# A dense SwiGLU trunk on one core: the down projection's first loads ahead of three products, their casts spread, and a bank order swapped

## The chip, the cores and the metric

The kernel runs on one core of one Trainium2 chip. The metric is the device time of one execution in microseconds, lower is better. TensorE (PE) multiplies, VectorE (DVE) and ScalarE (ACT) do elementwise work, GpSimd (POOL) does more of it from SBUF alone, and SyncE (SP) issues most of the transfers. TensorE writes into banks of PSUM, from which VectorE and ScalarE read.

## The reference

Two layers over a sequence of 1024 tokens of width 1024. Each layer has an attention part and a dense part. The change lies in the dense part:

```python
h = rmsnorm(x, norm_ffn[i])
gu = h @ w_gate_up[i]                                   # 1024 -> 2 * 2816
x = x + (silu(gu[..., :D_FF]) * gu[..., D_FF:]) @ w_down[i]   # 2816 -> 1024
```

All data are float32. The kernel keeps float32 accuracy by splitting every operand into a high part (a cast, on ScalarE, line L106) and a low part (operand minus high part, usually on VectorE, line L109), and runs three matmuls per product: high by high, high by low, low by high.

## The kernel before

**Gate and up.** The 22 column blocks of 128 are walked in pairs. `Pair(j)` is one block with its gate and up weights, and its share of the product is formed by a Strassen-like scheme of seven products, numbered 0 to 6, each of 12 matmuls of 128x512 (line L885). Results gather in two PSUM banks, X (products 0, 2, 4, 6) and Y (1, 3, 5). From block 4 on the seventh product of two neighbouring blocks is replaced by an object `Fourth`, which does it with a second Strassen step in quarters, split into three steps: "A", "B" and "C". Each step has six 128x256 matmuls per part (line L967), and gathers in two further banks, again named X and Y. So a pair (a, b) runs as a0 to a5, b0 to b3, A, b4, B, b5, C: the list `order`. After each product comes `read(n)`: for A and B two subtractions on VectorE (line L995), for C several more and the multiplication with the gate. A bank is written again only after its reading: A's banks by B, B's banks by C. `prepare` makes the weights of the product four steps ahead. After C, `hand_over` forms seven right-hand sides for the down projection and stores them in DRAM, `b_d` (line L1124).

**Down projection.** It, too, runs as seven products, numbered i, over the 11 pairs of rows, in six groups g of two rows (the last of one). For each (i, g):

- `keep_rows(g)` loads rows of the down weights (`wd_kept`, line L1178) once; they are kept for later products. Their tiles have tag "t8", six buffers, shared with operands of gate and up (the right sides of products 2, 3, and the one of A, B and C).
- `left_side(i, g)` casts these rows into high and low part (`wd`). These tiles share three buffers with the weights of gate and up.
- `right_side(i, g)` loads a piece of `b_d` into `b_raw` (line L1232) and casts its two halves into high and low part (`hB`). Both kinds of tile have tag "h", sixteen buffers, which the right sides of products 0, 1, 4 and 5 hold up to the last pair.

The matmuls of the down projection are line L1300.

**The order of the work.** `gate_up()` yields after each product with the number of products still to go, negative: -9 stands behind b0 of the last pair, -8 behind b1, -7 behind b2, -6 behind b3, -5 behind A, -4 behind b4, -3 behind B, -2 behind b5 and -1 behind C. At these places the loop below it starts the first groups of the down projection. The framework that builds the program puts each engine's instructions into one queue, in an order that it plans, and adds the semaphores; a tile gets its buffer in the order in which tiles of its tag are asked for.

Of the kernel before, what the change touches and what calls it, by code (L numbers as in the profile page):

```python
# [9 lines left out]
F32 = mybir.dt.float32  # L10
F32R = mybir.dt.float32r
AF = mybir.ActivationFunctionType
ALU = mybir.AluOpType
# [4 lines left out]
P = 128  # L18
# [3 lines left out]
HS = 512  # L22
# [19 lines left out]
def trunk_kernel(ctx: ExitStack, tc: tile.TileContext, a: dict, out: bass.AP):  # L42
# [21 lines left out]
    hp = pool("hp", bufs=16)  # L64
# [36 lines left out]
    def raw_tile(name):  # L101

        return phase[0].tile([P, D], F32, tag="raw", name=name, bufs=phase[2])

    def hi(dst, src):
        nc.scalar.copy(dst, src)  # L106
# [42 lines left out]
    def run_some(g, n):  # L149
        for _ in range(n):  # L150
            next(g, None)
# [119 lines left out]
    with tc.tile_pool(name="mp", bufs=1, reuse_waits="tile") as mp:  # L271
# [19 lines left out]
        for k in range(NK):  # L291
            t, g = mhl[:, k], gains[:, 4, k : k + 1]
# [24 lines left out]
        for i in range(8):  # L317
            l, u = divmod(i, 4)
# [47 lines left out]
    for layer in range(2):  # L366
        is_a = layer == 0
        with tc.tile_pool(name=f"ap{layer}", bufs=1, reuse_waits="tile") as ap:
# [385 lines left out]
            groups = 13  # L754
            for i in range(len(halves)):
# [12 lines left out]
                ahead = halves[min(i + 3, len(halves) - 1)].h  # L768
# [25 lines left out]
        with (  # L794
# [129 lines left out]
            h2 = HS // 2  # L924

            class Fourth:
# [45 lines left out]
                def product(self, n):  # L972
                    a11, a12, a22, s1, s2, s3, s4 = self.w
                    block = lambda k0, c: [
                        [B[6][k0 + k][:, i, c : c + h2] for i in range(2)] for k in range(2)
                    ]
                    b11, t1, b21, b22 = block(0, 0), block(0, h2), block(2, 0), block(2, h2)
                    t2, t3, t4 = ([[z[:, k] for z in t] for k in range(2)] for t in fourth)
                    if n == "A":
                        self.X = ps_t.tile([P, HS], F32, tag="T", name="X4")  # L980
                        self.Y = ps_o.tile([P, HS], F32, tag="O", name="Y4")
                        self.part(self.X, 0, a11, b11, start=True)
                        self.part(self.Y, 0, a12, b21, start=True)
                    elif n == "B":
                        self.part(self.X, 0, s2, t2)
                        self.part(self.Y, h2, s1, t1)
                    else:
                        self.part(self.X, 0, s3, t3)
                        self.part(self.Y, h2, s4, b22, stop=True)
                        self.part(self.X, h2, a22, t4, stop=True)  # L990

                def read(self, n):
                    (a, b), X, Y = self.units, self.X, self.Y
                    low, high = slice(0, h2), slice(h2, HS)
                    sub = lambda c, ps, op=ALU.subtract: nc.vector.tensor_tensor(c, c, ps, op=op)  # L995
                    if n == "A":
                        sub(a.c1[:, low], X[:, low])
                        sub(a.c1[:, low], Y[:, low])
                    elif n == "B":
                        sub(a.c1[:, high], X[:, low])  # L1000
                        sub(b.c1[:, high], Y[:, high])
                    else:
                        sub(
                            b.c1.rearrange("p (n c) -> p n c", n=2),
                            X[:, low].unsqueeze(1).to_broadcast([P, 2, h2]),
                        )
                        sub(a.c1[:, high], Y[:, high])
                        sub(b.c1[:, low], X[:, high], ALU.add)
                        for u in self.units:
                            sub(u.c1, u.g1, ALU.mult)  # L1010

            us = [Pair(j) for j in range(NF)]
            first = 4
# [14 lines left out]
            def load_gu():  # L1028
                u, i = next(loads, (None, 0))
                if u is not None:  # L1030
                    u.raw[i] = raw_tile("wgu_raw")
                    nc.sync.dma_start(u.raw[i], a["w_gu"][layer, 2 * u.j + i])
# [3 lines left out]
            for f in range(2):  # L1036
                for m in range(NK):
                    n = f * NK + m + 3
# [111 lines left out]
            def gate_up():  # L1150
                run_some(rest, 1)
                load_gu()
                for i, (u, n) in enumerate(order):
                    if i + lead < len(order):
                        v, n_ = order[i + lead]
                        v.prepare(n_)
                    u.product(n)
                    u.read(n)
                    run_some(rest, 1 if i < 2 * first else 2)
                    if i >= 7 * first - 1:  # L1160
                        run_some(more, 1)
                    if n == "C":
                        hand_over(u.units[0].j // 2, *u.units)
                    elif n == 6 and u.j % 2:
                        hand_over(u.j // 2, us[u.j - 1], u)
                    yield i - len(order)
# [3 lines left out]
            groups = [(p, min(2, HF - p)) for p in range(0, HF, 2)]  # L1170
# [5 lines left out]
            def rows(dst, g, i, cs):  # L1176
                p, n = groups[g]
                nc.sync.dma_start(dst, wd[p : p + n, i].rearrange("n r c -> r n c")[:, :, cs])  # L1178

            def keep_rows(g):  # L1180
                if g not in kept:
                    p, n = groups[g]
                    kept[g] = fp.tile([P, 2, 2, HS], F32, tag="t8", name="wd_kept", bufs=6)[:, :n]
                    rows(kept[g][:, :, 0], g, 0, slice(0, HS))

            def left_side(i, g):

                p, n = groups[g]
                first_cols, second_cols = slice(0, HS), slice(HS, D)

                def raw():
                    return raw_tile("wd_raw").rearrange("p (n c) -> p n c", c=HS)[:, :n]

                if i == 0:
                    keep_rows(g)
                a, b = kept[g][:, :, 0], kept[g][:, :, 1]
                if i == 0:
                    src = a
                elif i == 1:
                    src = raw()  # L1200
                    rows(src, g, 1, first_cols)
                elif i == 2:
                    nc.vector.tensor_tensor(a, b, a, op=ALU.subtract)
                    src = a
                elif i == 3:
                    r, o = raw(), raw()
                    rows(r, g, 0, second_cols)
                    rows(o, g, 1, second_cols)
                    nc.vector.tensor_tensor(b, r, o, op=ALU.add)
                    src = b  # L1210
                elif i == 4:
                    src, o = raw(), raw()
                    rows(src, g, 0, first_cols)
                    rows(o, g, 0, second_cols)
                    nc.vector.tensor_tensor(src, src, o, op=ALU.subtract)
                elif i == 5:
                    src = raw()
                    rows(src, g, 1, first_cols)
                    nc.vector.tensor_tensor(src, src, a, op=ALU.subtract)
                else:  # L1220
                    src = raw()
                    rows(src, g, 1, second_cols)
                w = wp.tile([P, 2, D], F32R, tag="whl", name="wd", bufs=3)
                hi(two(w[:, 0], n), src)
                lo(two(w[:, 1], n), src, two(w[:, 0], n))
                for q in range(n):
                    left[i, p + q] = w[:, :, q * HS : (q + 1) * HS]

            def right_side(i, g):
                p, n = groups[g]  # L1230
                raw = hp.tile([P, 2, HS], F32R, tag="h", name="b_raw").bitcast(F32)
                nc.sync.dma_start(  # L1232
                    raw[:, :n], b_d[layer][i][:, p * HS : (p + n) * HS].rearrange("r (n c) -> r n c", c=HS)
                )
                for q in range(n):
                    t = hp.tile([P, 2, HS], F32R, tag="h", name="hB")
                    hi(t[:, 0], raw[:, q])
                    lo(t[:, 1], raw[:, q], t[:, 0])
                    right[i, p + q] = t
# [65 lines left out]
            def finish(norm, at):  # L1305
# [23 lines left out]
                if last:  # L1329
                    nc.scalar.dma_start(out[:2].rearrange("k p t -> p k t")[:, :, at:], first)  # L1330

            for to_go in gate_up():
                if -7 <= to_go <= -5:
                    keep_rows(to_go + 7)
                    if to_go > -7:
                        left_side(0, to_go + 6)
                if -6 <= to_go <= -4:
                    right_side(0, to_go + 6)
            norms = [Norm(), Norm() if is_a else Norm(HS, 7)]
            dorder = [(i, g) for i in (0, 1, 3, 2, 4, 5, 6) for g in range(len(groups))]  # L1340
            parts = iter(())
# [1 line left out]
            for at_, (i, g) in enumerate(dorder):  # L1343
# [4 lines left out]
                p, n = groups[g]  # L1348
                if g == 0:
                    if i in (0, 6):  # L1350
                        X = banks(i)
# [114 lines left out]
```

## Time and profile before

| | us |
|---|---|
| median of 3 runs | 2156.2 |
| lowest, highest | 2154.42, 2159.33 |
| profiled execution, its own time | 2163.15 |
| span of the profiled execution | 2161.3 |

| engine | busy us | share of the span |
|---|---|---|
| PE | 2114.2 | 98% |
| PEld (weight loads, beside PE) | 1758.0 | 81% |
| DVE | 1514.0 | 70% |
| ACT | 1060.8 | 49% |
| POOL | 578.5 | 27% |

A row of the timeline has the start in us, the time, the engine, the line, the operation, the tiles written and read, the shapes and the count; a bracket has the engine's idle time before it and what ended that. Tiles are shown by name without number, so X, Y, `hB` and `wgu` stand for several tiles each; the line tells the products apart. The granted clock of TensorE is given as a share of full speed; its mean over the execution is 0.988.

### The profile page before, as it was taken

Reading aid. Unit: us, or ns where it says so; the run is one execution under the profiler, and the core shown is the slowest. Engines: PE = TensorE matmul, PEld = TensorE weight load, DVE = VectorE, ACT = ScalarE, POOL = GpSimd, SP = SyncE. Lnnn points to the kernel's source line nnn. Section 1 sums busy time; section 2 is a strip of 40 time slices with the busy share of each in tenths; the row PEclk is TensorE's granted clock in tenths of the full one; section 3 lists DMA queues with packets and bytes.
Section 4 is the critical chain, followed back from the end, with each engine's and each line's share of the span. In section 5 each row is a group of like instructions: output and inputs, shape, how many; then the busy total and the mean of one; then the engine's idle time right before and its main releaser. Section 6 shows DMA issues by size and latency. Waiting matters only on the chain. (4 is left out here: it accounts for less than half of the span.)

```text
span 2161.3 us, 28955 instructions
## 1 busy us (share of the span) xinstructions
PE 2114.2 (98%) x10270; PEld 1758.0 (81%) x10270; DVE 1514.0 (70%) x2466; ACT 1060.8 (49%) x2034; POOL 578.5 (27%) x617
## 2 busy tenths in 40 slices
PE   7999999999999999999999999999999999999997
PEld 6788888788888888888778888887888888878886
DVE  7677787788666666866766666677886666667675
ACT  6577785444433434334466566653543434344442
POOL 0344330334443430000233223203243444400000
PEclk9999999999999999999999999999999999999998
DMA  6321118323222336865232222274232333267662
GB/s 247 100 93 45 35 59 293 116 83 126 103 89 103 108 112 239 288 220 204 96 98 65 71 66 81 71 261 148 74 108 103 108 113 107 88 239 254 203 209 92
DMA packets 120081, 287.27 MB, mean 133 GB/s; under 512 B 12289, under 2 KB 18689, under 8 KB 119937
## 3 DMA queue, kind: packets, MB, share of 16 engines
q1 hardware_dynamic: 112896, 272.57, 37.4%
q10 hardware_dynamic: 7040, 12.85, 1.6%
q8 instruction: 81, 1.33, 0.3%
q14 instruction: 64, 0.52, 0.1%
HBM read 210.40 MB, written 68.94 MB: 129 GB/s over the span
## 5 line engine op out<-in xcount | busy, mean ns | idle before, releaser
L885 PE MATMUL Y<-hB,wgu 128*128 128x512 f32 x1056 | 261.6, 398 | 0.8 <-ACT c L905 0.8
L885 PE MATMUL X<-hB,wgu 128*128 128x512 f32 x1056 | 254.6, 390 | 0.0
L109 DVE TENSOR_TENSOR wgu<-wS,wgu 128x1024 fp32r<-128x1024 f32 (+1 forms) x124 | 153.4, 1237 | 130.5 <-ACT wgu L106 130.4
L1300 PE MATMUL X<-hB,wd 128*128 128x512 f32 x1056 | 242.3, 390 | 1.1 <-DVE x L1268 1.1
L885 PEld LDWEIGHTS Y<-hB,wgu 128*128 128x128 f32 x1056 | 200.4, 192 | 45.3 <-issue 1.9
L1300 PEld LDWEIGHTS X<-hB,wd 128*128 128x128 f32 x1056 | 197.9, 188 | 43.1 <-issue 2.4
L885 PEld LDWEIGHTS X<-hB,wgu 128*128 128x128 f32 x1056 | 196.1, 188 | 40.0
L587 POOL TENSOR_SCALAR p<-p,stat 128x384 f32<-128x384 f32 (+1 forms) x256 | 141.6, 573 | 313.1 <-DVE stat L584 203.7
L139 PE MATMUL mm<-hT,wqk 128*128 128x512 f32 x672 | 200.0, 405 | 0.1
L106 ACT CAST wgu<-wS 128x1024 fp32r<-128x1024 f32 (+1 forms) x124 | 114.3, 923 | 148.0 <-POOL wS L842 124.6
L139 PE MATMUL po<-yT,wo 128*128 128x512 f32 x768 | 184.6, 394 | 0.0
L1300 PE MATMUL Y<-hB,wd 128*128 128x512 f32 x792 | 180.4, 389 | 0.0
L233 POOL TENSOR_TENSOR nr<-nv,neg_half 128x4 f32<-128x4 f32 (+1 forms) x11 | 11.7, 1065 | 606.6 <-DVE nv L232 606.5
L1300 PEld LDWEIGHTS Y<-hB,wd 128*128 128x128 f32 x792 | 148.6, 188 | 31.1 <-DVE x L1268 0.3
L139 PEld LDWEIGHTS po<-yT,wo 128*128 128x128 f32 x768 | 142.4, 188 | 29.5 <-issue 1.0
L885 PE MATMUL X<-hT,wgu 128*128 128x512 f32 x624 | 150.2, 391 | 0.0
L842 POOL TENSOR_TENSOR wS<-wgu_raw 128x512 f32<-128x512 f32 x44 | 61.0, 1387 | 299.6 <-DVE wgu L109 299.6
L106 ACT CAST hB<-b_raw 128x512 fp32r<-128x512 f32 x154 | 88.9, 618 | 104.6 <-DMA b_raw<-b_d 87.4
L885 PEld LDWEIGHTS X<-hT,wgu 128*128 128x128 f32 x624 | 116.8, 188 | 26.3
L574 ACT ACTIVATE p<-p,stat 128x256 f32<-128x256 f32 (+1 forms) x192 | 112.4, 586 | 51.6 <-DVE stat L570 49.0
L109 DVE TENSOR_TENSOR pl<-pT,ph 128x384 fp32r<-128x384 f32 (+1 forms) x256 | 118.8, 494 | 21.3 <-ACT ph L106 18.4
L109 DVE TENSOR_TENSOR hB<-b_raw,hB 128x512 fp32r<-128x512 f32 x154 | 99.7, 687 | 46.9 <-ACT hB L106 46.9
(179 smaller groups left out, 4243.0 us busy)
## 6 DMA issues: line engine op xcount, KB each, us to landing
wgu_raw<-in_w_gu SPq DMA_DIRECT2D x92, 512.0 KB
wd_raw<-in_w_dn SPq DMA_DIRECT2D x70, 512.0 KB
b_raw<-b_d SPq DMA_DIRECT2D x70, 512.0 KB
b_d<-c SPq DMA_DIRECT2D x88, 256.0 KB
b_d<-t SPq DMA_DIRECT2D x66, 256.0 KB
wo_raw<-in_w_out SPq DMA_DIRECT2D x32, 512.0 KB
x<-in_x SPq DMA_DIRECT2D x32, 256.0 KB
xr_d<-x ACTq DMA_DIRECT2D x32, 256.0 KB
```

Of the source, the lines that this page charges most:

```text
L106: nc.scalar.copy(dst, src)
L109: (eng or nc.vector).tensor_tensor(dst, src, h.bitcast(F32), op=ALU.subtract)
L139: nc.tensor.matmul(ps[:, :n], l, r, start=start and i == 0 and j == 0, stop=stop and i == len(order) - 1 and j == 2,)
L233: nc.gpsimd.tensor_tensor(r[:, :nb], v[:, :nb], neg_half[:, :nb], op=ALU.pow)
L574: nc.scalar.activation(p[:, :n], p[:, :n], AF.Exp, bias=m1, scale=-1.0, accum_out=s1)
L587: nc.gpsimd.tensor_scalar(p[:, :n], p[:, :n], ri[:, i : i + 1], 1.0, op0=ALU.mult, op1=ALU.mult)
L842: sub = lambda o, p_, q_: nc.gpsimd.tensor_tensor(o, p_, q_, op=ALU.subtract)
L885: nc.tensor.matmul(ps, l, r, start=n in (0, 1, 3, 6) and k == 0 and i == 0, stop=k == 3 and i == 2, skip_group_check=True,)
L1300: nc.tensor.matmul(bank, l, r, start=i in (0, 1, 3, 6) and p == 0 and n == 0, stop=p == HF - 1 and n == 2, skip_group_check=True,)
```

## The change

Three edits.

1. In step C of `Fourth` the two parts that go to bank X run one after the other, and the part for bank Y comes last. `read("C")` follows: the two subtractions from X and the multiplication for block b first, then the subtraction from Y and the multiplication for block a.
2. `right_side` is split: `load_rows(i, g)` asks for the `b_raw` tile and starts its load; `right_side` does so only where it has not been done.
3. The start of the down projection within the last pair goes by a table. Before and after, by place:

| behind | before | after |
|---|---|---|
| b0 (-9) | | b_raw loads of groups 0 and 1 |
| b1 (-8) | | b_raw load of group 2 |
| b2 (-7) | kept rows 0 | kept rows 0, kept rows 1, casts of right side 0 |
| b3 (-6) | kept rows 1, left side 0, right side 0 | kept rows 2 |
| A (-5) | kept rows 2, left side 1, right side 1 | left side 0 |
| b4 (-4) | right side 2 | casts of right side 1 |
| B (-3) | | left side 1 |
| b5 (-2) | | casts of right side 2 |

```diff
                     else:
                         self.part(self.X, 0, s3, t3)
+                        self.part(self.X, h2, a22, t4, stop=True)
                         self.part(self.Y, h2, s4, b22, stop=True)
-                        self.part(self.X, h2, a22, t4, stop=True)
...
+                        sub(b.c1[:, low], X[:, high], ALU.add)
+                        sub(b.c1, b.g1, ALU.mult)
                         sub(a.c1[:, high], Y[:, high])
-                        sub(b.c1[:, low], X[:, high], ALU.add)
-                        for u in self.units:
-                            sub(u.c1, u.g1, ALU.mult)
+                        sub(a.c1, a.g1, ALU.mult)
...
-            def right_side(i, g):
+            raws = {}
+
+            def load_rows(i, g):
                 p, n = groups[g]
-                raw = hp.tile([P, 2, HS], F32R, tag="h", name="b_raw").bitcast(F32)
+                raws[i, g] = raw = hp.tile([P, 2, HS], F32R, tag="h", name="b_raw").bitcast(F32)
                 nc.sync.dma_start(
                     raw[:, :n], b_d[layer][i][:, p * HS : (p + n) * HS].rearrange("r (n c) -> r n c", c=HS)
                 )
+
+            def right_side(i, g):
+                p, n = groups[g]
+                if (i, g) not in raws:
+                    load_rows(i, g)
+                raw = raws.pop((i, g))
...
+            ahead = {
+                -9: [(load_rows, 0), (load_rows, 1)],
+                -8: [(load_rows, 2)],
+                -7: [(keep_rows, 0), (keep_rows, 1), (right_side, 0)],
+                -6: [(keep_rows, 2)],
+                -5: [(left_side, 0)],
+                -4: [(right_side, 1)],
+                -3: [(left_side, 1)],
+                -2: [(right_side, 2)],
+            }
             for to_go in gate_up():
-                if -7 <= to_go <= -5:
-                    keep_rows(to_go + 7)
-                    if to_go > -7:
-                        left_side(0, to_go + 6)
-                if -6 <= to_go <= -4:
-                    right_side(0, to_go + 6)
+                for what, g in ahead.get(to_go, ()):
+                    what(g) if what is keep_rows else what(0, g)
```

## The prediction

> **What bounds the kernel.** I read the page's busy shares first, then the timeline of TensorE where a pair of gate and up ends, then VectorE, ScalarE and SyncE there, and last the stretches with the granted clock.
>
> ```profile
> span 2161.3 us, 28955 instructions
> PE 2114.2 (98%) x10270; PEld 1758.0 (81%) x10270; DVE 1514.0 (70%) x2466; ACT 1060.8 (49%) x2034; POOL 578.5 (27%) x617
> ```
>
> TensorE bounds it; only time in which TensorE waits or runs slowly can be won. The next rows are TensorE at the last pair of layer 1: products A, b4 (L885, X), B (X, then Y), b5, C, and the first product of the down projection. Brackets are idle time and its releaser.
>
> ```profile
> 1915.00 0.88 PE L967 MATMUL X<-hT,wgu 128*128 128x256 f32 x6
> ...
> 1920.87 0.98 PE L967 MATMUL X<-q4h,wgu 128*128 128x256 f32 x6 [1.53 <-DVE c L995]
> 1923.89 1.65 PE L967 MATMUL Y<-hT,wgu 128*128 128x256 f32 x6 [2.05 <-DVE c L995]
> 1925.34 4.88 PE L885 MATMUL Y<-hB,wgu 128*128 128x512 f32 x12
> 1930.05 0.88 PE L967 MATMUL X<-q4h,wgu 128*128 128x256 f32 x6
> ...
> 1932.20 1.09 PE L1300 MATMUL X<-hB,wd 128*128 128x512 f32 x4
> ```
>
> From the start of A to the down projection: 1932.20 - 1915.00 = 17.20 us. The pair before it is the yardstick:
>
> ```profile
> 1876.88 0.88 PE L967 MATMUL X<-hT,wgu 128*128 128x256 f32 x6
> ...
> 1885.25 0.88 PE L967 MATMUL X<-q4h,wgu 128*128 128x256 f32 x6
> 1886.21 0.98 PE L967 MATMUL Y<-hT,wgu 128*128 128x256 f32 x6
> ...
> 1887.75 0.63 PE L885 MATMUL X<-hB,wgu 128*128 128x512 f32 x2
> ```
>
> A to C takes 1885.25 - 1876.88 = 8.37 us, and a C that waits for nothing 1932.20 - 1930.05 = 2.15. So 10.52 us would do, and the last pair of layer 1 loses 6.68. Layer 0 has the same place:
>
> ```profile
> 826.40 0.88 PE L967 MATMUL X<-hT,wgu 128*128 128x256 f32 x6
> ...
> 831.72 0.98 PE L967 MATMUL X<-q4h,wgu 128*128 128x256 f32 x6 [0.98 <-DVE c L995]
> 833.19 1.10 PE L967 MATMUL Y<-hT,wgu 128*128 128x256 f32 x6 [0.49 <-DVE c L995]
> ...
> 840.49 0.85 PE L1300 MATMUL X<-hB,wd 128*128 128x512 f32 x3
> ```
>
> 840.49 - 826.40 = 14.09: 3.57 lost. Why VectorE is late (layer 1; brackets name what ScalarE and VectorE waited for):
>
> ```profile
> 1914.06 0.57 ACT L902 COPY g<-X 128x512 f32<-128x512 f32 x1
> 1916.76 1.15 ACT L106 CAST hB<-b_raw 128x512 fp32r<-128x512 f32 x2 [2.14 <-DMA b_raw<-b_d]
> 1918.17 1.05 ACT L106 CAST wd<-wd_kept 128x1024 fp32r<-128x1024 f32 x1 [0.27 <-DMA wd_kept<-in_w_dn]
> 1919.13 0.58 ACT L905 COPY c<-Y 128x512 f32<-128x512 f32 x1
> 1919.26 1.23 DVE L109 TENSOR_TENSOR wd<-wd_kept,wd 128x1024 fp32r<-128x1024 f32 x1 [0.55 <-ACT wd L106]
> 1920.40 0.41 DVE L995 TENSOR_TENSOR c<-c,X 128x256 f32<-128x256 f32 x1
> 1921.20 1.05 ACT L106 CAST wd<-wd_kept 128x1024 fp32r<-128x1024 f32 x1 [1.50 <-DMA wd_kept<-in_w_dn]
> 1922.28 1.23 DVE L109 TENSOR_TENSOR wd<-wd_kept,wd 128x1024 fp32r<-128x1024 f32 x1 [1.47 <-ACT wd L106]
> 1923.42 0.41 DVE L995 TENSOR_TENSOR c<-c,Y 128x256 f32<-128x256 f32 x1
> 1923.75 0.69 DVE L893 TENSOR_TENSOR c<-c,c 128x512 f32<-128x512 f32 x1
> ```
>
> The subtractions that free A's two banks (L995) stand in VectorE's queue behind the low parts of group 0 and group 1 of the down projection's left side, which wait for ScalarE's casts, which wait for transfers. B may not overwrite the banks until then. The queues do not follow the program text: the copy L905 belongs to a product ahead of A, yet two casts written behind it run first. What counts is the built order, which I infer but cannot see: an operation seems to stand where its data were expected, and the data come later. SyncE's issues:
>
> ```profile
> 1904.76 0.93 SPq L1178 DMA_DIRECT2D wd_raw<-in_w_dn  x2
> 1905.79 0.42 SPq L1232 DMA_DIRECT2D b_raw<-b_d  x1
> 1909.25 0.34 SPq L1124 DMA_DIRECT2D b_d<-c  x1
> 1909.68 0.39 SPq L1249 DMA_DIRECT2D xr<-xr_d  x1
> 1910.15 0.42 SPq L1232 DMA_DIRECT2D b_raw<-b_d  x1
> 1911.11 3.09 SPq L1178 DMA_DIRECT2D wd_kept<-in_w_dn  x3
> 1914.25 0.46 SPq L1232 DMA_DIRECT2D b_raw<-b_d  x1
> ```
>
> The second b_raw was issued 4.4 us after the first, behind a store that waits for VectorE and a residual load. Last, the clock, and the transfers:
>
> ```profile
> 414.05:417.46 3.41, 2.51 (x16) 1.92 (x15) 2.12 (x3) 0.59 (x1) 3.04 (x2) 1.00 0.50 192
> 417.46:420.87 3.41, 3.41 (x9) 2.01 (x7) 0.69 (x1) 0.00 (x0) 1.02 (x1) 0.50 0.00 0
> 960.20:963.60 3.40, 2.35 (x11) 1.71 (x10) 3.40 (x6) 2.09 (x3) 0.00 (x0) 1.00 0.54 161
> 963.60:967.00 3.40, 3.40 (x17) 2.82 (x16) 3.19 (x5) 0.00 (x0) 0.00 (x0) 1.00 0.91 313
> 833.88:837.30 3.42, 3.42 (x11) 2.74 (x10) 1.72 (x4) 0.22 (x1) 0.00 (x0) 0.50 0.96 331
> 1919.00:1924.00 5.00, 1.42 (x9) 0.89 (x7) 3.28 (x5) 2.62 (x5) 0.00 (x0) 0.87 1.04 401
> ```
>
> Columns: stretch, us, busy PE, PEld, DVE, ACT, POOL, clock, DMA share, GB/s. Behind layer 0's stall TensorE runs at half clock for 3.42 us, which costs 1.7. A stretch with 3.41 - 2.51 = 0.90 us of idling (414.05) was followed by half clock, one with 3.40 - 2.35 = 1.05 (960.20) was not. The transfers are full at 401 GB/s: one of 0.52 MB takes 1.31 us.
>
> **C takes its second bank last.** In the yardstick C takes 1887.75 - 1885.25 = 2.50 us instead of 2.15: its Y part starts at 1886.21, 0.96 after the X part instead of 0.72. This grouped row (weight loads in layer 0's gate and up; layer 1's is the same) counts it:
>
> ```profile
> PEld Y L967 <- DVE c L995: 2.3, 8, 0.3
> ```
>
> 16 times 0.35 = 5.6 us. With both X parts first, Y starts at 1885.25 + 1.44 = 1886.69, 0.48 after the bank was free. Nothing else changes on TensorE. On VectorE the same five operations run in another order, b's bank first; who waits for them is hand_over and its stores to b_d, and in all pairs but the last those are read tens of us later, in the down projection. I take 5.6; bounds 0 (the late producer slips on with it) and 5.6.
>
> **The loads.** All three b_raw loads are written ahead of the pair's other transfers: two after b0, one after b1. Their slots come from operand tiles that b0 and b1 free one by one. Before, the second load's slot stood in line behind the first group's two cast tiles; now the three are next to each other. So on SyncE they should go out together near 1906, 0.42 us each in a queue idle until 1909.25, ahead of the store, the residual and the kept rows. The kept rows themselves wait for tiles that b2 and b3 free, so their issue at 1911.11 stays, whatever the text says. Bytes are the same. The three issues, 1.3 us together, are hidden in that idle stretch; if an operand tile came free late, SyncE would hold the store and the residual behind the waiting load, and neither is read before the down projection. The store's reader is group 5, the last. The change touches no queue of POOL.
>
> **The casts.** Right side 0 comes one product sooner, left side 0 behind A's read, the others later. ScalarE casts the three b_raw groups (3 * 1.15 us) in its idle time up to 1916, where today it stands 2.14 us waiting for the second; each low part follows on VectorE, which no one waits for there. Then I expect A's subtractions ahead of left side 0 on VectorE, so B starts when b4 ends. Gain up to 3.57 + 6.68 = 10.25 us. Late next: left side 1. Its kept rows landed at 1921.20 in layer 1; cast 1.05, low part 1.23, the addition that follows b4 (L893) 0.69 and B's subtraction 0.41 make 1924.6, while C would start at 1915.00 + 8.37 = 1923.37: 1.2 us of stall, and perhaps a half clock, 1.7. Layer 0 loses 3.1 us less today at the same queue order, so its transfers must come that much sooner, and I put its rest at none. Bounds of this rest: 0 to 2.9; I take 1.5, since 1.2 lies just above where the clock did and did not drop.
>
> In the Trainium skill ("TensorE: Matmul & The Clock Gate", Part 1: The HAM clock gate) the clock drops after an idle window of about 3.4 us. The trace disagrees: half clock followed 0.98 + 0.49 us of idling. By that rule the rest would be 1.2 and the sum 0.3 us larger.
>
> The skill's "DMA: Bandwidth & Descriptors" (Queues, rings and completion order) says that each engine consumes descriptors in ring order. That speaks against the change: the third b_raw, now ahead of the kept rows, would push them back by 1.31 us, and the sum would be that much smaller. In the trace the first kept rows landed only 1.4 us behind the second b_raw (1918.17 against 1916.76), which agrees; that they lose what the b_raw loads win is not shown.
>
> **Sum.** 5.6 + 10.25 - 1.5 = 14.35 us. The profiled execution took 2163.15 (span 2161.3), the median run 2156.2, so 6.95 less; where, no row tells. If a usual run loses in layer 1 what layer 0 loses, the gain is 5.6 + 2 * 3.57 = 12.7. Between the two, 13.2: 2156.2 - 13.2 = 2143.
>
> **Rivals.** (1) Nothing is left over in either layer: 15.85, 2140.4. For it: ScalarE and VectorE have idle time. Against: transfers are full.
> (2) Left side 0 still gets in front of one of A's subtractions. The kept rows land at 1918.17 at best; cast, low part and subtraction end at 1920.9, where Y of B should start at 1919.9 (b4 takes (8.37 - 4 * 0.72) / 2 = 2.75, so 1915.00 + 1.44 + 2.75 + 0.72): 1 us of stall and often a half clock, some 3 us in each layer. Gain 5.6 + 10.25 - 6 = 9.85: 2146.4. For it: today's order in both layers is exactly this.
> (3) The change does not do what it says: the built order stays and only C gains, 5.6: 2150.6.
> (4) Slower: ScalarE's queue gets the third b_raw's casts in front of the copy L902 (1914.06), which b4 needs at 1915.00 + 1.44 = 1916.44. With the 8.8 us that the second kept rows needed from issue to landing (the middle one of the three in that row, about 1912.4, to 1921.20), a b_raw issued at 1906.7 lands at 1915.5; casts 1.15 and copy 0.57 end at 1917.2: 0.8 of stall. It decides only if the two layers lose 15.85 + 4.3: 10 us each, a landing some 17 us after the issue. Then 2161. Against it: no transfer here took that long.
>
> **Chances.** Forecast 0.50 (its own range 2141 to 2146), (1) 0.13, (2) 0.20, (3) 0.10, (4) 0.07. Within 0.2% (4.3 us, about what this kernel's runs can tell) means 2151.9 to 2160.5: part of (3). Faster 0.83, same 0.10, slower 0.07. The range runs from below (1), 2138, to just past (3), 2152.
>
> **What would show it.** C's X, X, Y with no idle weight loads before Y; the b_raw issues close together near b0; A's two L995 rows ahead of every L109 row on wd; 10.5 to 11.5 us from A to L1300 in both layers; no half clock there. Wrong if an L106 cast with a transfer as releaser still precedes an eviction that TensorE needs, or if the late producers of B's second subtraction (the additions on POOL) slip with C.

## The result, and the profile after

The changed kernel takes 2144.63 us (median; 2144.17 to 2145.85) against 2156.63 us for the kernel before, timed on the same chip. The medians differ by 12.0 us. The ratio is 0.995, with a 95% interval of 0.9937 to 0.9962, and it stands for 10.8 us less, between 8.2 and 13.6; gains below are given by the ratio. The forecast was 2143, or 13.2 us less. The profiled execution took 2144.64 us, which is the median as well; the profiled execution of before lay 6.95 us above the median of 2156.2.

First the page of the changed kernel: span, and busy time of each engine.

```profile
span 2142.7 us, 28954 instructions
PE 2100.1 (98%) x10270; PEld 1749.9 (82%) x10270; DVE 1514.4 (71%) x2466; ACT 1062.1 (50%) x2034; POOL 577.2 (27%) x617
```

The five engines have the same numbers of instructions as before, and TensorE still bounds the kernel. Its busy time is 14 us less, as fewer of its matmuls run at half clock: the mean granted clock is 0.994, from 0.988. More than half of that isn't the change's: a second profiled execution of the kernel before (below) has 2106.3 us and a clock of 0.993. The waits of the weight loads for bank Y on the subtractions, over the whole trace (us in total, times, longest):

```profile
PEld Y L967 <- DVE c L995: 1.1, 2, 0.7
```

Two such waits on bank Y are left, both in a product B of a last pair, and one of 0.3 us on bank X, in layer 0's B. The prediction's row counted eight in one layer's gate and up; no C waits any more. Now TensorE at the last pair of layer 1, by its timeline: A, b4, B, b5, C, and the first product of the down projection (L1300 is L1308 now).

```profile
1902.36 0.88 PE L967 MATMUL X<-hT,wgu 128*128 128x256 f32 x6
...
1906.54 0.88 PE L967 MATMUL X<-q4h,wgu 128*128 128x256 f32 x6
1907.65 0.98 PE L967 MATMUL Y<-hT,wgu 128*128 128x256 f32 x6 [0.23 <-DVE c L995]
1908.47 2.92 PE L885 MATMUL Y<-hB,wgu 128*128 128x512 f32 x12
1911.23 1.60 PE L967 MATMUL X<-q4h,wgu 128*128 128x256 f32 x12
1912.66 0.88 PE L967 MATMUL Y<-hT,wgu 128*128 128x256 f32 x6
1913.38 2.00 PE L1308 MATMUL X<-hB,wd 128*128 128x512 f32 x8
```

C is X (twelve matmuls in one row), then Y, without a bracket: the swap does what was said. From A to the down projection are 1913.38 - 1902.36 = 11.02 us (17.20 before; 10.52 would do). B's X part starts as b4 ends; its Y part comes 0.39 us later than it should, 1907.65 - 1906.54 = 1.11 instead of 0.72. The same place in layer 0, and the clock behind it (the last row is a stretch, with the columns of the prediction's):

```profile
819.69 0.88 PE L967 MATMUL X<-hT,wgu 128*128 128x256 f32 x6
...
825.41 0.98 PE L967 MATMUL Y<-hT,wgu 128*128 128x256 f32 x6 [0.49 <-DVE c L995]
831.13 1.09 PE L1308 MATMUL X<-hB,wd 128*128 128x512 f32 x4
```

```profile
831.13:841.00 9.87, 9.87 (x46) 8.17 (x45) 7.77 (x14) 2.71 (x4) 0.00 (x0) 1.00 0.95 298
```

11.43 us by the starts before rounding (14.09 before), again with one wait at B's Y, and full clock behind it. So 0.50 and 0.91 us are left in the two layers. ScalarE and VectorE in layer 1 show why there is a wait at all:

```profile
1902.14 0.58 ACT L902 COPY g<-X 128x512 f32<-128x512 f32 x1
1903.48 1.05 ACT L106 CAST wd<-wd_kept 128x1024 fp32r<-128x1024 f32 x1 [0.25 <-DMA wd_kept<-in_w_dn]
...
1904.57 1.23 DVE L109 TENSOR_TENSOR wd<-wd_kept,wd 128x1024 fp32r<-128x1024 f32 x1 [0.60 <-ACT wd L106]
1904.92 1.05 ACT L106 CAST wd<-wd_kept 128x1024 fp32r<-128x1024 f32 x1
1905.71 0.42 DVE L995 TENSOR_TENSOR c<-c,X 128x256 f32<-128x256 f32 x1
1906.04 1.22 DVE L109 TENSOR_TENSOR wd<-wd_kept,wd 128x1024 fp32r<-128x1024 f32 x1
1907.18 0.42 DVE L995 TENSOR_TENSOR c<-c,Y 128x256 f32<-128x256 f32 x1
```

VectorE's order here is that of before, row by row: low part of left side 0, A's first subtraction, low part of left side 1, A's second subtraction. What differs is when the data are there. The first cast of kept rows starts 1903.48 - 1902.36 = 1.12 us behind A's start and the second 2.56; before it was 3.17 and 6.20 (1918.17 and 1921.20 against 1915.00). SyncE shows where that comes from:

```profile
1893.13 1.38 SPq L1234 DMA_DIRECT2D b_raw<-b_d  x3
...
1898.47 4.45 SPq L1178 DMA_DIRECT2D wd_kept<-in_w_dn  x4
...
1903.48 0.43 SPq L1257 DMA_DIRECT2D xr<-xr_d  x1
```

The three b_raw loads go out together, as forecast. The kept rows are issued 3.89 us ahead of A in both kernels (1902.36 - 1898.47 here, 1915.00 - 1911.11 before). Two things around them are new. The residual load `xr`, which stood ahead of them, is now behind four of them, which the prediction did not see. And the DMA engines are busier when the kept rows' issue begins. That stretch of 2 us, before and then after (share 0.90, then 1.05):

```profile
1910.10:1912.10 2.00, 2.00 (x11) 1.65 (x10) 0.00 (x0) 0.56 (x2) 0.00 (x0) 1.00 0.90 297
```

```profile
1897.45:1899.45 2.00, 2.00 (x11) 1.64 (x10) 0.31 (x1) 0.96 (x2) 0.00 (x0) 1.00 1.05 369
```

### The profile page after: what moved, and what is told of

Its sections match the earlier page's. It is cut to its first block, busy times and chain, and to the rows that moved or that the text cites. A ratio compares the mean times of both kernels' runs of the same rounds, so it can differ in the third digit from the quotient of the medians.

```text
span 2142.7 us, 28954 instructions
## 1 busy us (share of the span) xinstructions
PE 2100.1 (98%) x10270; PEld 1749.9 (82%) x10270; DVE 1514.4 (71%) x2466; ACT 1062.1 (50%) x2034; POOL 577.2 (27%) x617
## 4 chain that ended last, share of the span: by engine, by line
PE 77%; issue 13%; DVE 4%; ACT 3%; POOL 2%; DMA 1%; SPq 0%; DVEq 0%; ACTq 0%; POOLq 0%
PE X L885 16%; PE Y L885 16%; PE mm L139 14%; PE po L139 8%; PE X L1308 6%; PE Y L1308 4%; PE S L559 3%; PE O L622 3%; PE pT L602 3%; PE X L967 2%; PE Y L967 2%; ACT p L574 1%; DVE pl L109 1%; POOL wS L842 1%; DMA wm_raw<-in_w_mem 1%
## 5 line engine op out<-in xcount | busy, mean ns | idle before, releaser
L885 PE MATMUL Y<-hB,wgu 128*128 128x512 f32 x1056 | 256.1, 392 | 0.8 <-ACT c L905 0.8
L1308 PE MATMUL X<-hB,wd 128*128 128x512 f32 x1056 | 242.4, 390 | 1.1 <-DVE x L1276 1.1
L109 DVE TENSOR_TENSOR wgu<-wS,wgu 128x1024 fp32r<-128x1024 f32 (+1 forms) x124 | 152.9, 1233 | 124.9 <-ACT wgu L106 124.8
L1308 PEld LDWEIGHTS X<-hB,wd 128*128 128x128 f32 x1056 | 197.9, 188 | 43.2 <-issue 2.4
L1308 PE MATMUL Y<-hB,wd 128*128 128x512 f32 x792 | 180.4, 389 | 0.0
L1308 PEld LDWEIGHTS Y<-hB,wd 128*128 128x128 f32 x792 | 148.6, 188 | 31.2 <-DVE x L1276 0.3
L109 DVE TENSOR_TENSOR pl<-pT,ph 128x384 fp32r<-128x384 f32 (+1 forms) x256 | 118.7, 494 | 21.0 <-ACT ph L106 17.9
L109 DVE TENSOR_TENSOR hB<-b_raw,hB 128x512 fp32r<-128x512 f32 x154 | 100.0, 688 | 42.3 <-ACT hB L106 42.0
```

The source lines that it names most:

```text
L109: (eng or nc.vector).tensor_tensor(dst, src, h.bitcast(F32), op=ALU.subtract)
L885: nc.tensor.matmul(ps, l, r, start=n in (0, 1, 3, 6) and k == 0 and i == 0, stop=k == 3 and i == 2, skip_group_check=True,)
L1308: nc.tensor.matmul(bank, l, r, start=i in (0, 1, 3, 6) and p == 0 and n == 0, stop=p == HF - 1 and n == 2, skip_group_check=True,)
```

## The experiments

Every kernel was timed beside the kernel before on its own chip. "The last pair" below is the time from A's start to the down projection, layer 0 then layer 1; it is taken before rounding, so that a difference of two rows shown can be 0.01 off. After the result I held two theories of the last pair: its loss fell because the kept rows land sooner (early data), or what counts is that A's subtractions stand behind low parts on VectorE, and a change of that order alone would do as much (order).

**The swap alone.** Edit 1 of the diff, and nothing else.

```diff
+                        self.part(self.X, h2, a22, t4, stop=True)
                         self.part(self.Y, h2, s4, b22, stop=True)
-                        self.part(self.X, h2, a22, t4, stop=True)
```

> The kernel before with the bank order of step C alone. If the swap is worth what the prediction says, C takes 2.15 us instead of 2.50 in the 16 pairs that waited, and the time falls by 5.6 us, while the last pair still takes 14 to 17 us from A to the down projection. If the late producer of B's second subtraction only slips along with C, the time falls by less than 2 us and the weight loads of Y keep their wait.

2151.07 us; ratio 0.9974 [0.9964, 0.9984], which is 5.6 us (3.5 to 7.8). Waits of the weight loads on L995 in its trace, then the last pair of layer 1 by the timeline of TensorE, and the clock over it:

```profile
PEld X L967 <- DVE c L995: 3.7, 2, 2.5
PEld Y L967 <- DVE c L995: 1.4, 2, 0.7
```

```profile
1902.06 0.88 PE L967 MATMUL X<-hT,wgu 128*128 128x256 f32 x6
1908.44 0.97 PE L967 MATMUL X<-q4h,wgu 128*128 128x256 f32 x6 [2.03 <-DVE c L995]
1909.90 0.98 PE L967 MATMUL Y<-hT,wgu 128*128 128x256 f32 x6 [0.50 <-DVE c L995]
```

```profile
1908.00:1916.00 8.00, 7.07 (x44) 6.33 (x45) 6.25 (x12) 4.18 (x8) 0.00 (x0) 1.00 0.94 345
```

All four waits stand in the two B's; no C waits. From the first A of a layer's gate and up to its last, TensorE takes 302.4 us in both layers, against 305.0 to 305.1 in the two traces of the kernel before: 5.3 to 5.4 us, read from the traces alone. The last pair takes 12.33 and 13.57 us, less than the 14 to 17 expected: its loss is still there, but layer 1 loses 3.05 with the old loads and not 6.68. And 2.03 + 0.50 us of idling were not followed by half clock.

**The loads alone.** The changed kernel without the swap, and with the casts at their old places.

```diff
                 -9: [(load_rows, 0), (load_rows, 1)],
                 -8: [(load_rows, 2)],
-                -7: [(keep_rows, 0), (keep_rows, 1), (right_side, 0)],
-                -6: [(keep_rows, 2)],
-                -5: [(left_side, 0)],
-                -4: [(right_side, 1)],
-                -3: [(left_side, 1)],
-                -2: [(right_side, 2)],
+                -7: [(keep_rows, 0)],
+                -6: [(keep_rows, 1), (left_side, 0), (right_side, 0)],
+                -5: [(keep_rows, 2), (left_side, 1), (right_side, 1)],
+                -4: [(right_side, 2)],
```

> The kernel before with the three b_raw loads asked for behind b0 and b1, the casts and the kept rows left at their old places, no swap. If the gain of the last pair comes from the transfers (early loads fill a stretch in which the DMA was not full, so the kept rows land earlier), the last pair takes 10.8 to 11.6 us from A to the down projection, and the time falls by about 12.0 - 5.6 = 6.4 us. If it comes from where the casts stand in the text, the last pair stays above 13 us and the time falls by less than 3 us.

2152.91 us; ratio 0.9981 [0.9970, 0.9992], 4.1 us. The timeline of ScalarE and TensorE, layer 1:

```profile
1908.85 0.88 PE L967 MATMUL X<-hT,wgu 128*128 128x256 f32 x6
1910.12 1.05 ACT L106 CAST wd<-wd_kept 128x1024 fp32r<-128x1024 f32 x1
...
1914.28 0.98 PE L967 MATMUL Y<-hT,wgu 128*128 128x256 f32 x6 [0.38 <-DVE c L995]
```

The kept rows' cast starts 1.27 us behind A without a wait for the transfer, and the last pair takes 11.39 and 11.14 us, as in the changed kernel. Together with the swap's 5.6 this makes 9.7 of the 10.8. The time fell by less than the 6.4 that I had expected, which was what the swap leaves of the medians' 12.0; the interval, 1.7 to 6.5 us, just contains it.

**The casts alone.** The table of the changed kernel without its two rows of `load_rows`, and no swap.

```diff
-                -9: [(load_rows, 0), (load_rows, 1)],
-                -8: [(load_rows, 2)],
```

> The kernel before with the casts and the kept rows at their new places, but each b_raw load asked for with its casts as before, no swap. If the transfers are the cause, nothing changes: within 2 us of the kernel before, and A's second subtraction still behind both low parts of the left side. If the spreading is the cause (the prediction's step), A's subtractions are ahead of the left side, and the time falls by 5 us or more.

2156.66 us; ratio 0.9994 [0.9985, 1.0003]: nothing. The last pair takes 14.35 and 11.77. VectorE in layer 0:

```profile
826.61 1.22 DVE L109 TENSOR_TENSOR wd<-wd_kept,wd 128x1024 fp32r<-128x1024 f32 x1 [1.38 <-ACT wd L106]
827.75 0.41 DVE L995 TENSOR_TENSOR c<-c,X 128x256 f32<-128x256 f32 x1
828.08 1.22 DVE L109 TENSOR_TENSOR wd<-wd_kept,wd 128x1024 fp32r<-128x1024 f32 x1
829.22 0.41 DVE L995 TENSOR_TENSOR c<-c,Y 128x256 f32<-128x256 f32 x1
```

A's second subtraction still stands behind both low parts. Writing the casts elsewhere in the text left the queue at this place as it was: only the low parts of right side 2 moved, behind B's subtractions.

**The casts alone, with the order forced.** The kernel above, but the low part of left side 0 must be issued behind A's second subtraction, and that of left side 1 behind B's second. The calls for the transfers stand elsewhere in the text, but SyncE issues them in the order of the kernel before, and at the same times from A's start. This run sets the order against the early data.

```diff
-                        sub(a.c1[:, low], Y[:, low])
+                        marks["A"] = sub(a.c1[:, low], Y[:, low]).ins
...
-                        sub(b.c1[:, high], Y[:, high])
+                        marks["B"] = sub(b.c1[:, high], Y[:, high]).ins
...
-                lo(two(w[:, 1], n), src, two(w[:, 0], n))
+                behind = marks.pop("AB"[g], None) if i == 0 and g < 2 else None
+                with tc.issue_after(behind) if behind is not None else ExitStack():
+                    lo(two(w[:, 1], n), src, two(w[:, 0], n))
```

> Like the kernel with the casts alone, but with the order on VectorE forced: the low part of left side 0 behind A's second subtraction, that of left side 1 behind B's second. Old loads, no swap. If the loss of the last pair is one of order in VectorE's queue, TensorE no longer waits at B, and only C may wait for the second kept rows (landing about 6.2 us behind A's start in layer 1, then cast 1.05, copy 0.58, addition 0.69, subtraction 0.41: 0.6 us late): 10.5 to 11.2 us from A to the down projection, the time 6 to 9 us lower. If late transfers are the whole cause, the wait moves on to C and the last pair stays above 13 us.

2152.18 us; ratio 0.9979 [0.9968, 0.9989], 4.5 us. The last pair takes 11.15 and 10.53 us. ScalarE, VectorE and TensorE in layer 1:

```profile
1911.61 0.88 PE L967 MATMUL X<-hT,wgu 128*128 128x256 f32 x6
1914.29 1.05 ACT L106 CAST wd<-wd_kept 128x1024 fp32r<-128x1024 f32 x1 [0.22 <-DMA wd_kept<-in_w_dn]
1914.79 0.41 DVE L995 TENSOR_TENSOR c<-c,X 128x256 f32<-128x256 f32 x1
1915.30 0.42 DVE L995 TENSOR_TENSOR c<-c,Y 128x256 f32<-128x256 f32 x1
1915.64 1.22 DVE L109 TENSOR_TENSOR wd<-wd_kept,wd 128x1024 fp32r<-128x1024 f32 x1
1915.79 0.88 PE L967 MATMUL X<-q4h,wgu 128*128 128x256 f32 x6
```

The kept rows land late as before (the cast starts 2.68 us behind A), and yet B does not wait, since A's subtractions are ahead of the low part. So in this layer the late landing of the kept rows costs only through the order. In layer 0, B's X part still comes about 0.5 us late, for a reason that the last run below shows. I had expected 6 to 9 us of gain; its basis, 6.68 in layer 1, was too large.

**The changed kernel with the order forced**: the same edit of `marks` on the changed kernel.

> The changed kernel with the order on VectorE forced: low part of left side 0 behind A's second subtraction, that of left side 1 behind B's second. If the rest of the loss (11.44 and 11.02 us from A to the down projection, instead of 10.52) comes from the two low parts that still stand ahead of A's second subtraction, both become 10.5 to 10.6 and the time falls by 0.9 + 0.5 = 1.4 us against the changed kernel. If it comes from the transfers, C waits instead and nothing is gained.

2144.73 us; ratio 0.9945 [0.9933, 0.9957]. Layer 1, by the timeline of VectorE:

```profile
1905.19 0.42 DVE L995 TENSOR_TENSOR c<-c,Y 128x256 f32<-128x256 f32 x1
1905.53 1.22 DVE L109 TENSOR_TENSOR wd<-wd_kept,wd 128x1024 fp32r<-128x1024 f32 x1
```

The last pairs take 10.53 and 10.52 us, and TensorE has no wait on L995 left in the trace. Against the changed kernel in the same group of runs (next) that is 0.1 us by the medians and 1.3 us by the ratios, whose intervals overlap: the 1.4 us that I expected can be read in the trace, but the time can't tell.

**The changed kernel again**, for a second execution with a profile.

> The changed kernel once more, for the comparison with the forced order on the same chip and for a second trace: 2144 to 2146 us, 11.0 to 11.5 us from A to the down projection in both layers. If the half clock comes by chance where the idling falls in a fixed raster of 3.41 us, the stretches at half clock near 410 and 1493 us can be there in this trace; if the change itself removed them, they are absent again.

2144.83 us; ratio 0.9951 [0.9937, 0.9964]. The last pair takes 11.61 and 11.09 us, the first casts of kept rows start 1.72 and 1.20 us behind A: like the first trace. The clock is full from 96 to 2130 us in both traces. That doesn't show that the change removed the half clock near 410 and 1493 us, since the loads alone, without the swap, have none there either, and the one near 417 comes and goes in the kernel before (below).

**The residual load ahead of the kept rows again.** This was to tell whether the kept rows land sooner because the b_raw loads start sooner, or because `xr` no longer stands ahead of them. The changed kernel, with

```diff
-                -8: [(load_rows, 2)],
+                -8: [(load_rows, 2), (first_residual, 0)],
```

> The changed kernel with the first residual load asked for behind b1, so that its 0.5 MB goes out ahead of the kept rows, as it did before the change; the three b_raw loads stay early. If the kept rows came sooner because this load was pushed behind them, they land 0.7 to 1.3 us later again, and the last pair takes 12 to 13 us. If it is the early start of the b_raw loads (more bytes moved by the time A starts), the last pair stays below 11.8 us.

2145.33 us; ratio 0.9947 [0.9934, 0.9960]. SyncE and VectorE in layer 1:

```profile
1895.29 0.41 SPq L1257 DMA_DIRECT2D xr<-xr_d  x1
1899.16 3.09 SPq L1178 DMA_DIRECT2D wd_kept<-in_w_dn  x3
...
1904.84 0.42 DVE L995 TENSOR_TENSOR c<-c,Y 128x256 f32<-128x256 f32 x1
1905.28 1.22 DVE L109 TENSOR_TENSOR wd<-wd_kept,wd 128x1024 fp32r<-128x1024 f32 x1
```

`xr` goes out ahead, but the planner also put A's subtractions ahead of the low parts and the store to `b_d` behind three kept rows. The last pair takes 10.53 us in both layers, for the reason of the forced order, so the 12 to 13 that early data alone would explain could not show. What can be read is the landing: the first casts of kept rows start 2.11 and 1.15 us behind A, against 1.56 and 1.12. One load more ahead of them cost 0 to 0.55 us, less than expected; but this load was issued 7.8 us ahead of A, against 5.3 in the kernel before. How much of the earlier landing is due to each of the two reasons stays open.

**The kernel before again**, for a second profiled execution of it.

> The kernel before once more, for a second trace: ratio 1.000 within 0.2%. If the half clock away from the last pairs (about 55 to 62, 417 to 421 and 1506 to 1510 us in the first trace, some 6.8 us lost) comes by chance, one or more of the three are absent and the profiled time is lower by 1.7 us for each stretch of 3.41 us that is missing. If it belongs to the kernel, all three are there again.

2157.14 us; ratio 1.0003 [0.9994, 1.0012]. Its profiled execution took 2155.76. TensorE in layer 1, then two stretches of the clock:

```profile
1911.35 0.88 PE L967 MATMUL X<-hT,wgu 128*128 128x256 f32 x6
1916.62 0.98 PE L967 MATMUL X<-q4h,wgu 128*128 128x256 f32 x6 [0.94 <-DVE c L995]
...
1923.81 1.55 PE L1300 MATMUL X<-hB,wd 128*128 128x512 f32 x6
```

```profile
55.60:62.40 6.80, 6.80 (x30) 5.12 (x31) 4.88 (x10) 1.50 (x3) 1.85 (x1) 1.00 0.48 164
417.50:420.90 3.40, 3.40 (x17) 2.74 (x16) 3.40 (x6) 1.52 (x3) 0.00 (x0) 1.00 0.00 0
```

The same program at the same place takes 1923.81 - 1911.35 = 12.46 us here (12.47 before rounding) and 17.20 in the execution on which the prediction was made; layer 0 takes 14.68 (14.09). The difference of 4.7 in layer 1 is idling, 1.53 + 2.05 in the prediction's rows against 0.94 + 0.49 (2.15 us), and half clock, which stretched B's Y part from 0.98 to 1.65 and b5 to 4.88 from the 2.92 that it takes in the changed kernel (2.6 us). Around 417.5, where the prediction's row shows half clock, the clock is full; so it is 3.1 us earlier, where this execution has the same matmuls, since it is full from 96 to 829 us. It is also full from 55.6 to 62.4, where the first trace of before had this:

```profile
55.60:62.40 6.80, 6.80 (x20) 5.54 (x20) 2.99 (x6) 0.27 (x1) 1.85 (x1) 0.50 0.43 140
```

The third stretch that I asked for, 1506.3 to 1509.7 us in the first trace, is there again: half clock from 1502.2 to 1505.6, at the same place of the program.

**Swap and forced order, without the early loads.** The kernel of the forced order, with edit 1.

> The kernel before with the bank order of C, the casts at their new places and the order on VectorE forced (left side 0 behind A's second subtraction, left side 1 behind B's), but with each b_raw load asked for with its casts as before. If order and early loads are two cures of one loss, the early loads are not needed here: 10.5 to 11.2 us from A to the down projection in both layers, and the time is that of the changed kernel, ratio 0.994 to 0.996. If the early loads bring something of their own, the time stays 1.5 us or more above the changed kernel, ratio 0.996 or more.

2145.09 us; ratio 0.9951 [0.9937, 0.9965]. The last pair takes 10.74 and 11.08 us. TensorE and VectorE, layer 1:

```profile
1900.95 0.88 PE L967 MATMUL X<-hT,wgu 128*128 128x256 f32 x6
1905.58 0.98 PE L967 MATMUL X<-q4h,wgu 128*128 128x256 f32 x6 [0.29 <-DVE c L995]
1903.90 1.29 DVE L109 TENSOR_TENSOR hB<-b_raw,hB 128x512 fp32r<-128x512 f32 x2 [4.33 <-ACT hB L106]
```

With the transfers issued in the order of the kernel before, this kernel is as fast as the changed one within the intervals. Early loads and forced order are two cures of one loss, and the second adds nothing that the time shows once the first is there. The forced order leaves 0.22 and 0.56 us: A's first subtraction (1905.11) stands behind the low parts of right side 1, shown last, whose casts on ScalarE waited 3.13 us for their b_raw load. The early loads remove these, as the changed kernel with the order forced shows. The last pairs of all traces side by side:

| kernel | layer 0 | layer 1 |
|---|---|---|
| before | 14.09 | 17.20 |
| before again | 14.68 | 12.47 |
| swap alone | 12.33 | 13.57 |
| casts alone | 14.35 | 11.77 |
| loads alone | 11.39 | 11.14 |
| changed | 11.43 | 11.02 |
| changed again | 11.61 | 11.09 |
| residual first | 10.53 | 10.53 |
| changed, order forced | 10.53 | 10.52 |
| casts alone, order forced | 11.15 | 10.53 |
| swap, order forced | 10.74 | 11.08 |

## Why the prediction was right and wrong

**The swap** was right: 5.6 us forecast, 5.6 (3.5 to 7.8) measured alone, 5.3 to 5.4 read from its trace, and no C waits. Its bound of 0 (the late producer slips on) did not come about.

**The loads** were right in their own step: three issues together, and the kept rows' issue unmoved. The step missed that the residual load would change sides with the kept rows. The loads alone bring the last pair to where the changed kernel has it, and the casts alone do not, so the gain in the pair is theirs.

**The casts** are the step that failed: "Then I expect A's subtractions ahead of left side 0 on VectorE". The first of them stayed between the two low parts and the second behind both, and the casts alone brought nothing. Nor were ScalarE's casts spread: in the changed kernel it casts all three right sides ahead of the first kept rows. The low parts of the right sides were said to be work "which no one waits for there"; with the swap and the forced order A's first subtraction waits behind them. "What would show it" asked for both L995 rows ahead of every L109 row on `wd`, and neither layer has that. Rival (2) had this order right. It put the stall at 1 us and "often a half clock", some 3 us in each layer; it measured 0.50 and 0.91, without half clock. It took the kept rows to land as late as before (cast at A + 3.17), and they came at A + 1.12 and 1.56. So the forecast came out near for a reason other than the one it gave, and that is luck: the measured interval, 8.2 to 13.6 us, holds the 9.85 of rival (2) as well as its own 13.2.

**The rest** of 1.5 us was expected at C, behind the kept rows of left side 1. It measured 0.50 + 0.91 = 1.4 and stands at B's Y part, where A's second subtraction waits for that same low part. The size held, the place did not, and forcing the order removes it.

**The term that was mis-sized** is 10.25 us for the last pairs, of which 6.68 in layer 1. The four traces with the old loads and the old order take 13.86 us in layer 0 and 13.75 in layer 1 on average, 3.3 and 3.2 above 10.52. Then the sum is 5.6 + 6.6 - 1.4 = 10.8 us. That it meets the measured gain so closely is chance: the four go from 11.77 to 17.20 in layer 1, and the gain is known to 8.2 to 13.6. The prediction had weighed the case that "a usual run loses in layer 1 what layer 0 loses", got 12.7 (without taking off the rest), and went to 13.2, between the two. One trace had 6.68 and 3.57 for the same order of work, and that disagreement was the warning.

**The 6.95 us** between the profiled execution and the median of before, "where, no row tells": the second execution of before is 7.4 us shorter in span. Put side by side matmul by matmul, it gains 2.9 us from 55.6 to 62.4 and 0.8 from 417.5 to 430, where its half clock is absent, 4.1 in the last pairs and some 0.5 in small steps, and loses 1.0 in the down projection of layer 1. Half of the length of a stretch at half clock (3.4 and 1.7 us) was too much for these two.

**The clock.** Half clock had followed 0.98 + 0.49 us of idling before; it did not follow 2.03 + 0.50 with the swap alone, nor 0.94 + 0.49 in layer 1 of the second execution of before. The Trainium skill ("TensorE: Matmul & The Clock Gate", Part 1: The HAM clock gate) has a drop after an idle window of about 3.4 us. The trace of before disagrees with that as a threshold, since no such idling stands ahead of its drop; the same section calls the window free-running, and that a short stall is sometimes followed by a drop and sometimes not, in one program, agrees with it. Whether the window's position decides was not tried.

**The transfers.** The third b_raw load ahead of the kept rows did not push them back by 1.31 us: their first cast came sooner in both layers (A + 1.56 and 1.12, from A + 2.63 and 3.17). The Trainium skill ("DMA: Bandwidth & Descriptors", Queues, rings and completion order) has descriptors consumed in ring order on each engine, and I had drawn the 1.31 from that; with the residual load ahead the kept rows came 0 to 0.55 us later, so the runs do not show that sum. The rule itself is neither confirmed nor denied, since the load that stood ahead started sooner too.

**Rivals (3) and (4).** (3) was half right, for the order on VectorE did stay. Of (4) the part about ScalarE came about, without its price: the copy L902 waits behind casts of b_raw and ends at 1902.72, about 1 us ahead of b4's need (1902.36 + 1.44 = 1903.80).

## What to carry to other kernels

When an eviction that TensorE needs stands behind work that waits for a transfer, there are two cures, sooner data or a forced order of issue, and one is enough; moving the call in the text may leave the built queue as it is, so read the order on the engine, not in the text. Before a stall goes into a sum, look at the same stall in a second execution, or at its twin in the other layer: here one place took 12.47 and 17.20 us in two executions of one program. Where two places with the same order of work disagree by a factor of two, don't add the larger until another trace decides; here the smaller was the usual one.

## What the runs showed of the hardware

- Half clock at one place of one program comes and goes between executions: from 55.6 to 62.4 us the clock was 0.50 in one and 1.00 in the other, which are 0.06 us apart in the program where the stretch begins; TensorE did 20 matmuls in it in one and 30 in the other. With a longer last pair, this put one profiled execution 7 us above its median.
- The landing of the same transfers in one program varies: in layer 1 the first cast of kept rows, which waited for its load in both executions of before, started 3.17 us behind A in one and 2.58 in the other. The second started at 6.20 us, 1.50 of it spent waiting for its load, and at 4.01 without such a wait. With the old order this went into TensorE's waits.
